# The first stage's order: a modulation half ahead of the norm's sums, first products between two modulation halves

## The chip, the cores and the metric

The kernel runs on 1 core of one Trainium2 chip. A core has TensorE (PE; its weight loads are listed apart as PEld), VectorE (DVE), ScalarE (ACT), GpSimd (POOL) and SyncE (SP), each with its own queue of instructions that it works off in order, and 16 DMA engines. The metric is the device time of one execution in microseconds; the time of a kernel is the median of its runs.

## The reference, cut to what matters

The program is one inference step of a two-layer diffusion backbone: 512 latent tokens and 128 context tokens with 1024 features go through the same weights. Both groups are modulated by their own condition vector. What the changed part computes is the very beginning of layer 0:

```python
def ada_modulation(cond, w_mod, b_mod):
    m = jax.nn.silu(cond) @ w_mod + b_mod
    return jnp.split(m, 6, axis=-1)

def modulate(h, shift, scale):
    return h * (1.0 + scale) + shift

hp = modulate(rms_norm(xp, norm_mix[l]), sh1_p, sc1_p)   # context tokens
hs = modulate(rms_norm(xs, norm_mix[l]), sh1_s, sc1_s)   # latent tokens
p = h @ w_in          # even_project: the first projection of the mixer
```

Behind it come the attention of layer 0, a SwiGLU feed-forward, layer 1 with grouped-query attention, a second feed-forward and a last norm. All inputs and outputs are float32.

## The kernel before

Activations are held transposed: 8 tiles of 128 features by 640 tokens (`x`, written x0 to x7), the tokens in two halves of 320 columns, `HALF`. The second half has 192 latent and 128 context tokens, and as the two have different conditions, its elementwise work is done in two pieces, of 192 and of 128 columns. A product at nearly float32 precision is made of three fast matmuls: an operand is split into a high part (`h`, rounded to the fast format by ScalarE) and a low part (`l`, the rest, by VectorE), and high x high, high x low and low x high are summed in PSUM (`mm3`, L181). `unit` (L168) loads a weight block of 128 x 1024 and splits it so: ScalarE's copy, then VectorE's subtraction (L173, L174).

The first stage, with the names that the profile shows:

- The norm (`nrm`, names n00...). ScalarE squares the x tiles (n00sq), VectorE adds them up (n00acc), `rstd(i)` (L215) sums over the features of half i with a matmul against ones (n00p), and ScalarE makes 1/sqrt of it by Ln and Exp (n00rs, L221 and L222).
- The modulation blocks `mod0(j)` (L353), names mod, for j = 0 to 3. A block gives shift and scale of the two feature tiles 2j and 2j+1 for both conditions. It has two halves, each of which multiplies 1 MB of weights (mraw, fetched in 2 DMAs per block) by the conditions (scol), 16 matmuls as the profile counts them; after the second half ScalarE copies the sums out of PSUM (modsb, L371), and `end()` turns them with matmuls against a selection matrix (sel) and adds the bias on VectorE (mods, L379).
- `made(j)` (L543) calls that end, makes the scale column (gs, L386) and then the modulated tiles 2j and 2j+1 for both halves: VectorE scales (h00t, L253), ScalarE adds the shift and rounds (h00h, L257), VectorE makes the low part (h00l, L258).
- `first(ks, us)` (L520) adds the products of the tiles ks with the weight blocks wA0, wA1 and wA4 (us = 0, 1, 2) to six PSUM banks, wA0a and wA0b, wA1a and wA1b, and two called wA. For one tile and one block that is 6 matmuls of 128 x 320.

The loads stand in one queue of SyncE: vectors, the 8 x tiles, block 0's two halves, wA0, block 1's two halves, wA1, wA4, the halves of blocks 2 and 3. The loads behind those (tabK, wA2, wA3 and so on) go out when buffers come free.

The order of the work is that in which the program text issues it, loosened by a scheduler that settles each engine's queue when the program is built. `run` (L115) binds its pieces: each is issued after the matmul that was written last before it. The order of this stage is written out by hand:

```python
nrm.rstd(0)
run([lambda: nrm.rstd(1)] + rows(0))
run([lambda: made(0)] + rows(1))
run([lambda: first((0, 1), [0]), lambda: made(1), lambda: first((0, 1), [1, 2])])
run(rows(2))
```

`rows(j)` (L551) are the two halves of block j. So TensorE has the norm's sums of both halves, block 0's two halves, block 0's end, block 1's two halves, the 12 products of tiles 0 and 1 with wA0, block 1's end, their 24 products with wA1 and wA4, and block 2.

Of the kernel before, what the change touches and what calls it, by code (L numbers as in the profile page):

```python
# [51 lines left out]
def body(ctx, tc, xT, vecs, crow, wm0, wm0g1, wm0g, wm1, wA, wNV, wNA, wMK, wMV, wOA, wGQ, wGK, wGV, wOC,  # L52
# [36 lines left out]
    def bank(name, kind="m"):  # L89
        if kind == "m":  # L90
            return psp.tile([P, 512], F32, tag="m", bufs=4, name=name)
        return ypool["pool"].tile([P, 512], F32, tag=kind, bufs=ypool["tags"][kind], name=name)
# [22 lines left out]
    def run(pieces):  # L115

        for piece in pieces:
            with tc.issue_after(PE.last.ins):
                piece()
# [48 lines left out]
    def unit(src, n, name, lo="v", pool=None, bufs=3):  # L168

        raw = load(src, n, name + "r")  # L170
        t = (pool or wp).tile([P, 2, 1024], F32R, tag="w", bufs=bufs, name=name)
        hi, lw = t[:, 0, :n], t[:, 1, :n]
        S.activation(hi, raw, AF.Copy)  # L173
        (V if lo == "v" else G).tensor_tensor(lw, raw, f(hi), ALU.subtract)  # L174
        return hi, lw
# [12 lines left out]
    def proj(ps, wh, wl, hh, hl, ks, c0, c1, first=True, last=True, w0=0):  # L188

        for j, k in enumerate(ks):  # L190
            a, b = wh[:, (w0 + j) * P:(w0 + j + 1) * P], wl[:, (w0 + j) * P:(w0 + j + 1) * P]
            mm3(ps[:, :c1 - c0], a, b, hh[k][:, c0:c1], hl[k][:, c0:c1], first and j == 0, last and j == len(ks) - 1)
# [160 lines left out]
    def mod0(j, bk, load_):  # L353

        box = []

        def part(half):
            def run():
                if half == 0:
                    box.append(bk())  # L360
                psm, rs = box[0], load_(j, half)

                for g in range(4):
                    for b in range(2):
                        o = 512 * (g % 2) + 256 * b
                        rows = slice(64 * b + 32 * (g % 2), 64 * b + 32 * (g % 2) + 32)
                        PE.matmul(psm[rows, :256], scol[:, 4 * half + g, :], rs[g // 2][:, o:o + 256], start=half == 0 and g < 2,
                                  stop=half == 1 and g > 1, tile_position=(0, rows.start))
                if half == 1:
                    box.append(tp.tile([P, HT], F32, tag="u", bufs=7, name=f"modsb{j}"))  # L370
                    S.activation(box[1][:, :256], psm[:, :256], AF.Copy)  # L371
            return run

        def end():
            psm, sb = box
            for i in range(2):
                PE.matmul(psm[:, 4 * i:4 * i + 4], sb[:, i * P:(i + 1) * P], sel, start=True, stop=True)
            for i, t in enumerate(MOD0[j]):
                V.tensor_tensor(mods[0][:, t:t + 2, :], psm[:, 0:8].rearrange("p (a i b) -> p a i b", a=2, b=2)[:, :, i, :],  # L379
                                bc2(bmod(0, t, 2)), ALU.add)  # L380
        return [part(0), part(1), end]

    def mkgs(l, i, k0=0, k1=8):
        sc = SC1 if i == 0 else SC2
        n = (V_NMIX if i == 0 else V_NFFN) + 8 * l
        V.scalar_tensor_tensor(gs[l][i][:, k0:k1, :], mods[l][:, sc + k0:sc + k1, :], 1.0, bc2(vec[:, n + k0:n + k1]),  # L386
                               ALU.add, ALU.mult)
# [119 lines left out]
    nrm = Norm("n00", D)  # L507
# [12 lines left out]
    def first(ks, us):  # L520
        for k in ks:
            for u in us:
                for c, (c0, c1) in enumerate(HALF):
                    proj(pss[u][c], *w3[u], hh, hl, [k], c0, c1, first=k == 0, last=k == KT - 1, w0=k)

    with tc.tile_pool(name="start", bufs=1) as big:
        raws = {}

        def fetch(j):
            for half in range(2):  # L530
                raws[j, half] = big.tile([P, 2, 1024], F32, tag="mraw", bufs=8, name=f"mraw{j}_{half}")
                nc.sync.dma_start(raws[j, half], wm0[j, 2 * half:2 * half + 2].rearrange("q p n -> p q n"))


        fetch(0)
        w3 = [unit(wA[0], 1024, "wA0")]
        fetch(1)
        w3 += [unit(wA[i], 1024, f"wA{i}") for i in (1, 4)]
        fetch(2)
        fetch(3)  # L540
        m = [mod0(j, lambda j=j: bank(f"mod{j}", "m"), lambda j, half: [raws[j, half][:, q, :] for q in range(2)]) for j in range(4)]

        def made(j):  # L543

            m[j][2]()
            mkgs(0, 0, 2 * j, 2 * j + 2)
            for k in (2 * j, 2 * j + 1):
                for i in range(2):
                    hm.make(i, nrm.rs, k)

        def rows(j):  # L551
            return m[j][:2]

        nrm.rstd(0)
        run([lambda: nrm.rstd(1)] + rows(0))
        run([lambda: made(0)] + rows(1))
        run([lambda: first((0, 1), [0]), lambda: made(1), lambda: first((0, 1), [1, 2])])
        run(rows(2))
        run([lambda: first((2, 3), [0]), lambda: made(2), lambda: first((2, 3), [1, 2])])
        run(rows(3))  # L560
        run([lambda: first((4, 5), [0]), lambda: made(3), lambda: first((4, 5), [1, 2])])
        run([lambda u=u: first((6, 7), [u]) for u in range(3)])
# [1530 lines left out]
```

## Time and profile before

| | |
|---|---|
| median of 3 runs | 1477.95 us |
| the 3 runs | 1477.95, 1478.81, 1476.01 us |
| profiled execution: span | 1475.7 us (its own time; no time around the span is listed) |
| TensorE busy | 1440.4 us, 98% |
| VectorE busy | 1235.6 us, 84% |
| ScalarE busy | 783.4 us, 53% |
| GpSimd busy | 176.0 us, 12% |
| HBM | 156 GB/s over the span; 413 GB/s from 10 to 20 us |
| first matmul of the norm's sums | at 13.52 us |
| first product of the first stage (wA0a) | at 23.72 us |
| block 2's first matmul | at 30.79 us |

Times inside the profile count from the span's start. In a timeline row stand start, duration, engine, line, operation, out<-in, the tile's size, xcount, and in brackets the idle time before it with what ended it; a row with xcount merges neighbours of one kind. A busy TensorE row overlaps the next, since matmuls are pipelined: 0.31 us is the duration of a 128 x 320 product, while such products follow each other every 0.15 us.

### The profile page before, as it was taken

The page shows a single profiled execution, that of the slowest core. Times are in us where ns is not written, and L with a number is a line of the kernel's source. Part 1 is how long each engine was busy: PE and PEld are TensorE (multiplying, and loading weights), DVE is VectorE, ACT ScalarE, POOL GpSimd, SP SyncE. Part 2 cuts the span into 40 slices and gives each one's busy share as a digit, 9 for nine tenths or more (in the row PEclk, how much of TensorE's full clock was granted, in tenths as well). Part 3 has the DMA queues.
Part 4 walks back from the last instruction along what each step waited for, and adds up shares of the span by engine and source line. Part 5 has one row for each costly group of instructions (what it writes and reads, how often), then busy time and mean ns, then how long its engine had stood idle before and what let it go on. Part 6 is the DMA issues. An engine that isn't in the chain of part 4 may idle for free.

```text
span 1475.7 us, 25826 instructions
## 1 busy us (share of the span) xinstructions
PE 1440.4 (98%) x9764; PEld 1390.5 (94%) x9764; DVE 1235.6 (84%) x2391; ACT 783.4 (53%) x1539; POOL 176.0 (12%) x270
## 2 busy tenths in 40 slices
PE   5999999999999999999999999999999999999997
PEld 3989978889999999999999999989999999999997
DVE  5877788877998889965997878888899898989976
ACT  5446677853755545531223656672656555555443
POOL 0046635420000000000000122220000000000000
PEclk9999999999999999999999999999999999999999
DMA  9643431025164555568764300115245555548572
GB/s 374 217 153 125 144 115 44 15 90 182 48 214 164 169 167 173 183 232 315 240 224 143 100 30 30 43 39 190 86 167 181 182 175 184 176 145 297 181 267 72
DMA packets 79637, 231.49 MB, mean 157 GB/s; under 512 B 8856, under 2 KB 13240, under 8 KB 79128
## 3 DMA queue, kind: packets, MB, share of 16 engines
q1 hardware_dynamic: 77152, 225.43, 44.8%
q10 hardware_dynamic: 1944, 3.48, 0.7%
q8 instruction: 76, 1.25, 0.3%
q0 software_dynamic: 416, 0.93, 0.2%
q14 instruction: 49, 0.40, 0.1%
HBM read 193.15 MB, written 36.66 MB: 156 GB/s over the span
## 4 chain that ended last, share of the span: by engine, by line
PE 75%; DVE 11%; DMA 5%; ACT 5%; issue 3%; POOL 1%; DVEq 0%; ACTq 0%; SPq 0%; POOLq 0%
PE fg L64 14%; PE fd L64 6%; PE fgo L64 5%; PE fo L64 5%; PE gq L64 4%; PE fu L64 3%; PE fdo L64 2%; PE gs L64 2%; PE go L64 2%; PE nq L64 2%; PE nk L64 1%; PE fuo L64 1%; DVE junk L1660 1%; PE gt L68 1%; DMA wm<-in_wm 1%
## 5 line engine op out<-in xcount | busy, mean ns | idle before, releaser
L1660 DVE SCALAR_TENSOR_TENSOR junk<-wm,cb 128x1024 bf16<-128x1024 f32 x88 | 107.3, 1220 | 6.7 <-DMA wm<-in_wm 5.5
L64 PE MATMUL gq<-h10h,wgq 128*128 128x320 f32 x256 | 66.3, 318 | 0.0
L267 POOL TENSOR_SCALAR h10h<-h10t,gs,mods 128x320 fp32r<-128x320 f32 x4 | 4.0, 992 | 430.8 <-DVE h10t L261 428.5
L1400 ACT ACTIVATE wY<-s 128x1024 fp32r<-128x1024 f32 x38 | 40.3, 1061 | 25.7 <-PE fg L64 21.1
L1928 POOL TENSOR_TENSOR xr<-xw,fn1rs 128x320 f32<-128x320 f32 x2 | 1.7, 858 | 412.9 <-ACT fn1rs L235 412.9
L1400 ACT ACTIVATE wZ<-s 128x1024 fp32r<-128x1024 f32 x38 | 40.1, 1055 | 15.4 <-PE fd L64 10.3
L1401 DVE TENSOR_TENSOR wZ<-s,wZ 128x1024 fp32r<-128x1024 f32 x38 | 46.3, 1220 | 1.4
L1401 DVE TENSOR_TENSOR wY<-s,wY 128x1024 fp32r<-128x1024 f32 x38 | 46.3, 1219 | 0.3
L64 PEld LDWEIGHTS gq<-h10h,wgq 128*128 128x128 f32 x256 | 45.3, 190 | 0.6
L1509 DVE TENSOR_TENSOR sg<-up,sg 128x640 f32<-128x640 f32 x38 | 31.3, 823 | 15.8 <-ACT sg L1508 14.8
L1508 ACT ACTIVATE sg<-fg 128x320 f32<-128x320 f32 x38 | 16.7, 439 | 48.4 <-PE fg L64 48.4
L64 PE MATMUL gq<-h10l,wgq 128*128 128x320 f32 x128 | 39.8, 311 | 0.0
L1530 ACT ACTIVATE p<-fd 128x320 f32<-128x320 f32 x38 | 16.6, 438 | 42.5 <-PE fd L64 42.5
L1865 ACT ACTIVATE gp<-gs,gb,rq 128x640 f32<-128x640 f32 (+1 forms) x40 | 31.8, 796 | 13.4 <-DVE gb L1864 12.0
L64 PE MATMUL fg<-h01E,wW 128*128 128x320 f32 x228 | 36.6, 309 | 1.1 <-DVE g L1540 1.1
L64 PE MATMUL fg<-h01N,wZ 128*128 128x320 f32 x228 | 36.6, 309 | 0.3 <-ACT p L1528 0.3
L64 PE MATMUL fg<-h01C,wY 128*128 128x320 f32 x228 | 36.6, 309 | 0.2 <-ACT u L1534 0.2
L64 PE MATMUL fg<-h11N,wZ 128*128 128x320 f32 x228 | 36.7, 309 | 0.0
L64 PE MATMUL fg<-h01q,wX 128*128 128x320 f32 x228 | 36.7, 309 | 0.0
L64 PE MATMUL fu<-h11q,wX 128*128 128x320 f32 x228 | 36.6, 309 | 0.0
L64 PE MATMUL fd<-h11q,wZ 128*128 128x320 f32 x228 | 36.6, 309 | 0.0
L64 PE MATMUL fd<-h01q,wZ 128*128 128x320 f32 x228 | 36.5, 309 | 0.0
(3421 smaller groups left out, 5313.5 us busy)
## 6 DMA issues: line engine op xcount, KB each, us to landing
wm<-in_wm SPq DMA_DIRECT2D x48, 512.0 KB, 4.3
mraw<-in_wm SPq DMA_DIRECT2D x8, 1024.0 KB, 13.2
mraw<-in_wm SPq DMA_DIRECT2D x14, 512.0 KB, 3.7
wmv<-in_wm0g SPq DMA_DIRECT2D x8, 512.0 KB, 4.0
wm<-in_wm0g SPq DMA_DIRECT2D x8, 512.0 KB, 5.4
ruo<-in_wFO SPq DMA_DIRECT2D x8, 512.0 KB, 4.1
rgo<-in_wFO SPq DMA_DIRECT2D x8, 512.0 KB, 5.5
x<-in_xT SPq DMA_DIRECT2D x8, 320.0 KB, 5.2
```

Of the source, the lines that this page charges most:

```text
L64: cls.last = nc.tensor.matmul(*a, **k)
L68: cls.last = nc.tensor.transpose(*a, **k)
L267: G.tensor_scalar(h[:, c0:c1], t, self.gsl[:, k, 0:1], self.ml[:, self.sh + k, 0:1], ALU.mult, ALU.add)
L1400: S.activation(h, src, AF.Copy)
L1401: V.tensor_tensor(w_, src, f(h), ALU.subtract)
L1508: last = S.activation(sg[:, 0:HT], g[:, :HT], AF.Silu, scale=-1.0)
L1509: V.tensor_tensor(sg, up, sg, ALU.mult)
L1530: S.activation(p5, b5[:, :HT], AF.Copy)
L1660: V.scalar_tensor_tensor(junk, raw, 1.0, cb[:, c, :], ALU.mult, ALU.mult, accum_out=mods[l][:, j0 + i, c:c + 1])
L1865: gexp[h, j] = S.activation(dst, src, AF.Exp, bias=nb, scale=rq[:, j:j + 1], accum_out=ll[:, j:j + 1])
L1928: G.tensor_tensor(x[k][:, c0:c1], root[1][k], nrm.rs[:, c0:c1], ALU.mult)
```

## The change

Four lines become six. The first half of block 0 is issued before the norm's sums of either half of the tokens. Block 1's second half is issued behind the six products of tile 0 with wA0, which `first((0,), [0])` makes right after block 1's first half; `first((1,), [0])` follows it with tile 1. No instruction is added, taken away or resized.

```diff
         def rows(j):
             return m[j][:2]
 
+        r0, r1 = rows(0), rows(1)
+        r0[0]()
         nrm.rstd(0)
-        run([lambda: nrm.rstd(1)] + rows(0))
-        run([lambda: made(0)] + rows(1))
-        run([lambda: first((0, 1), [0]), lambda: made(1), lambda: first((0, 1), [1, 2])])
+        run([lambda: nrm.rstd(1), r0[1]])
+        run([lambda: made(0), r1[0], lambda: first((0,), [0]), r1[1]])
+        run([lambda: first((1,), [0]), lambda: made(1), lambda: first((0, 1), [1, 2])])
         run(rows(2))
```

The queues as built differ in this stage on TensorE, ScalarE and VectorE; those of GpSimd and SyncE are the same, and so is everything behind the first 53 rows of VectorE. The numbers behind a name tell buffers apart.

**The head.** TensorE's queue from its first matmuls to block 0's selection matmuls; mraw_0 and mraw_1 are the weights of a block's first and second half. Before (-) and now (+):

```order
 L68 MATMUL cst<-ident,scol 8x128 x2
-L64 MATMUL n00p_239<-n00acc,ones 128x320
-L64 MATMUL n00p_243<-n00acc,ones 128x320
-L64 MATMUL mod_247<-mraw_0_208,scol 32x256 x8
-L64 MATMUL mod_247<-mraw_1_210,scol 32x256 x8
-L64 MATMUL mod_247<-sel,modsb_264 128x4 x2
+L64 MATMUL mod_239<-mraw_0_208,scol 32x256 x8
+L64 MATMUL n00p_248<-n00acc,ones 128x320
+L64 MATMUL n00p_252<-n00acc,ones 128x320
+L64 MATMUL mod_239<-mraw_1_210,scol 32x256 x8
+L64 MATMUL mod_239<-sel,modsb_264 128x4 x2
```

The first half of block 0 has moved ahead of both sums of the norm. ScalarE's queue at the same place, from the norm's Ln to block 0's copy and the first h00h; before:

```order
L221 ACTIVATE n00rs<-n00p_239,eps 128x320
L222 ACTIVATE n00rs<-n00rs 128x320
L221 ACTIVATE n00rs<-n00p_243,eps 128x320
L222 ACTIVATE n00rs<-n00rs 128x320
L371 ACTIVATE modsb_264<-mod_247 128x256
L173 ACTIVATE wA_214<-wA0r 128x1024
L257 ACTIVATE h00h_183<-h00t_271,mods_98 128x320
```

and now:

```order
L221 ACTIVATE n00rs<-n00p_248,eps 128x320
L222 ACTIVATE n00rs<-n00rs 128x320
L221 ACTIVATE n00rs<-n00p_252,eps 128x320
L173 ACTIVATE wA_214<-wA0r 128x1024
L222 ACTIVATE n00rs<-n00rs 128x320
L371 ACTIVATE modsb_264<-mod_239 128x256
L257 ACTIVATE h00h_183<-h00t_271,mods_98 128x320
```

The high part of wA0 (wA_214) has moved ahead of the norm's last Exp and of the copy modsb.

**The second block.** TensorE's queue from block 1's halves (mraw_0_217, mraw_1_219) to the first product of tile 1 (h00h_184); before:

```order
L64 MATMUL mod_293<-mraw_0_217,scol 32x256 x8
L64 MATMUL mod_293<-mraw_1_219,scol 32x256 x8
L64 MATMUL wA0a<-h00h_183,wA_214 128x320
L64 MATMUL wA0a<-h00l_191,wA_214 128x320
L64 MATMUL wA0a<-h00h_183,wA_214 128x320
L64 MATMUL wA0b<-h00h_183,wA_214 128x320
L64 MATMUL wA0b<-h00l_191,wA_214 128x320
L64 MATMUL wA0b<-h00h_183,wA_214 128x320
```

and now:

```order
L64 MATMUL mod_293<-mraw_0_217,scol 32x256 x8
L64 MATMUL wA0a<-h00h_183,wA_214 128x320
L64 MATMUL wA0b<-h00h_183,wA_214 128x320
L64 MATMUL wA0a<-h00l_191,wA_214 128x320
L64 MATMUL wA0a<-h00h_183,wA_214 128x320
L64 MATMUL wA0b<-h00l_191,wA_214 128x320
L64 MATMUL wA0b<-h00h_183,wA_214 128x320
L64 MATMUL mod_293<-mraw_1_219,scol 32x256 x8
```

Block 1's second half has moved behind the six products of tile 0. VectorE's queue at the end of tile 1 (h00l_192) and the start of block 1's scale and shift; wA_223 and wA_228 are the low parts of wA1 and wA4. Before:

```order
L258 SCALAR_TENSOR_TENSOR h00l_192<-h00t_286,mods_98,h00h_184 128x128
L174 TENSOR_TENSOR wA_223<-wA1r,wA_223 128x1024
L379 TENSOR_TENSOR mods_98<-mod_293,vec 128x4 x2
L386 SCALAR_TENSOR_TENSOR gs_100<-mods_98,vec 128x4
L174 TENSOR_TENSOR wA_228<-wA4r,wA_228 128x1024
L253 SCALAR_TENSOR_TENSOR h00t_329<-x_2_127,gs_100,n00rs 128x320
```

and now:

```order
L258 SCALAR_TENSOR_TENSOR h00l_192<-h00t_286,mods_98,h00h_184 128x128
L379 TENSOR_TENSOR mods_98<-mod_293,vec 128x4 x2
L386 SCALAR_TENSOR_TENSOR gs_100<-mods_98,vec 128x4
L253 SCALAR_TENSOR_TENSOR h00t_329<-x_2_127,gs_100,n00rs 128x320
L174 TENSOR_TENSOR wA_223<-wA1r,wA_223 128x1024
L258 SCALAR_TENSOR_TENSOR h00l_193<-h00t_329,mods_98,h00h_185 128x320
L253 SCALAR_TENSOR_TENSOR h00t_333<-x_2_127,gs_100,n00rs 128x192
L174 TENSOR_TENSOR wA_228<-wA4r,wA_228 128x1024
```

The low parts of wA1 and wA4 have moved behind block 1's mods and gs and behind the first one and three steps of tile 2. The low part of wA0, which stood between the first h00t and the first h00l, now stands ahead of block 0's mods.

## The prediction, on record before the changed kernel ran

> **What bounds the kernel now.** I read the busy sums first, then who waited for whom on TensorE, then the timelines of the first 33 us engine by engine. The table of stretches says that TensorE is the bound:
>
> ```profile
> 0.00:50.00 50.00, 33.91 (x282) 26.33 (x283) 29.62 (x87) 27.02 (x60) 0.70 (x6) 1.00 0.91 341
> 30.00:40.00 10.00, 10.00 (x106) 8.17 (x109) 8.07 (x26) 4.79 (x13) 0.00 (x0) 1.00 1.03 407
> 50.00:100.00 50.00, 50.00 (x270) 44.63 (x270) 45.78 (x76) 21.81 (x40) 13.27 (x26) 1.00 0.57 182
> sum 1475.70, PE 1440.38 PEld 1390.54 DVE 1235.59 ACT 783.45 POOL 175.97; mean PE 48.01 PEld 46.35 DVE 41.19 ACT 26.11 POOL 5.87
> PE n00p L64 <- DVE n00acc L212: 8.3, 1, 8.3
> ```
>
> In a row stand the stretch, its length, then the busy time of TensorE, its weight loads, VectorE, ScalarE and GpSimd with their instructions. TensorE is busy 1440.38 of 1475.70 us; of the 35.3 idle, 16.1 lie in the first 50 us (50-33.91), and from 30 us on it is busy 10.00 of 10. The changed region ends where the third modulation block starts; what counts is when that start comes, since behind it TensorE has no gap to give or take. Before it stands the start-up, where TensorE waits for VectorE, for DMA and for the split of weight block wA1. TensorE there:
>
> ```profile
> 13.52 2.50 PE L64 MATMUL n00p<-n00acc,ones 128*128 128x320 f32 x4 [8.30 <-DVE n00acc L212]
> 15.95 2.31 PE L64 MATMUL mod<-mraw,scol 128*32 128x256 f32 x32
> 18.77 0.61 PE L64 MATMUL mod<-sel,modsb 128*128 128x4 f32 x4 [0.51 <-ACT modsb L371]
> 20.25 1.07 PE L64 MATMUL mod<-mraw,scol 128*32 128x256 f32 x16 [0.87 <-DMA mraw<-in_wm]
> 22.72 1.07 PE L64 MATMUL mod<-mraw,scol 128*32 128x256 f32 x16 [1.40 <-DMA mraw<-in_wm]
> 27.38 0.41 PE L64 MATMUL wA1a<-h00h,wA 128*128 128x320 f32 x1 [0.36 <-DVE wA L174]
> 29.27 0.56 PE L64 MATMUL wA<-h00h,wA 128*128 128x320 f32 x2
> 30.79 1.93 PE L64 MATMUL mod<-mraw,scol 128*32 128x256 f32 x32
> ```
>
> Each row is start, length, what. 30.79 is the mark that I move.
>
> **Step 1, TensorE's head.** The first half of block 0 (16 matmuls) now stands ahead of the norm's sums n00p. Nothing is added; the work is the same. But TensorE works in order, so the sums now wait for that half's weights:
>
> ```profile
> 5.59 1.27 SPq L532 DMA_DIRECT2D mraw<-in_wm  x2
> mraw<-in_wm SPq DMA_DIRECT2D x1, 1024.0 KB, 8.1
> 7.88 0.34 SPq L165 DMA_DIRECT2D wA0r<-in_wA  x1
> wA0r<-in_wA SPq DMA_DIRECT2D x1, 512.0 KB, 9.7
> ```
>
> Issued at 5.59 and 8.1 us on the way, the half lands at 13.7; the sums could have begun at 13.52. So the half fills no idle TensorE time: the idle time that it was to fill ends before the data comes. What it costs depends on TensorE's speed at that moment:
>
> ```profile
> L64 PE MATMUL n00p<-n00acc,ones x4: 741/741/900, 13.5 to 15.3; 128*128 128x320 f32 x4
> L64 PE MATMUL cqp<-cqacc,ones x4: 432/432/433, 66.0 to 66.8; 128*128 128x320 f32 x4
> 65.96 1.24 PE L64 MATMUL cqp<-cqacc,ones 128*128 128x320 f32 x4
> ```
>
> The same four matmuls take 2.50 us at 13.5 and 1.24 us at 66: the array begins at half speed, although the granted clock reads 1.00 there. Both halves take 1.93 us at 30.79 and 2.31 at 15.95, so full speed came less than a microsecond into that row, at about 16.8. A half is therefore worth 0.86 us at full speed ((1.93-0.2)/2) and 1.7 at half. I take 1.7, since nothing warms the array earlier than before: 13.75+1.7 puts the sums at 15.5 instead of 13.52, +1.95; the low end is 14.6, +1.1. [...]
>
> **Step 2, ScalarE.** Its rows:
>
> ```profile
> 14.99 0.53 ACT L221 ACTIVATE n00rs<-n00p,eps 128x320 f32<-128x320 f32 x1 [2.21 <-PE n00p L64]
> 16.06 0.53 ACT L221 ACTIVATE n00rs<-n00p,eps 128x320 f32<-128x320 f32 x1
> 16.62 0.47 ACT L222 ACTIVATE n00rs<-n00rs 128x320 f32<-128x320 f32 x1
> 18.34 0.38 ACT L371 ACTIVATE modsb<-mod 128x256 f32<-128x256 f32 x1 [1.25 <-PE mod L64]
> 18.62 1.05 ACT L173 ACTIVATE wA<-wA0r 128x1024 fp32r<-128x1024 f32 x1
> 24.75 0.36 ACT L371 ACTIVATE modsb<-mod 128x256 f32<-128x256 f32 x1
> ```
>
> The first Ln follows the sums by 14.99-13.52 = 1.47, so 16.95. The split of wA0 now stands ahead of the last Exp: 16.95+1.07+0.56 = 18.58 (its weights land at 7.88+9.7 = 17.58, no wait), then 1.05+0.47 with a little overlap, and the copy modsb starts at 20.05 instead of 18.34: +1.7. TensorE's second half of block 0 (17.3 to 18.3) lies beside this. Were the sums not late, the split would wait for 17.58 and modsb still start at 19.1.
>
> **Step 3, VectorE.**
>
> ```profile
> 19.48 0.23 DVE L379 TENSOR_TENSOR mods<-mod,vec 128x4 f32<-128x4 f32 x2 [5.61 <-ACT modsb L371]
> 20.74 1.22 DVE L174 TENSOR_TENSOR wA<-wA0r,wA 128x1024 fp32r<-128x1024 f32 x1
> 21.87 0.55 DVE L258 SCALAR_TENSOR_TENSOR h00l<-h00t,mods,h00h 128x320 fp32r<-128x320 f32 x1
> 22.33 0.35 DVE L253 SCALAR_TENSOR_TENSOR h00t<-x,gs,n00rs 128x128 f32<-128x128 f32 x1
> 22.60 0.41 DVE L258 SCALAR_TENSOR_TENSOR h00l<-h00t,mods,h00h 128x192 fp32r<-128x192 f32 x1
> 22.93 0.55 DVE L253 SCALAR_TENSOR_TENSOR h00t<-x,gs,n00rs 128x320 f32<-128x320 f32 x1
> 23.65 0.68 DVE L253 SCALAR_TENSOR_TENSOR h00t<-x,gs,n00rs 128x192 f32<-128x192 f32 x2
> 24.24 1.14 DVE L258 SCALAR_TENSOR_TENSOR h00l<-h00t,mods,h00h 128x320 fp32r<-128x320 f32 x3
> 26.10 1.23 DVE L174 TENSOR_TENSOR wA<-wA1r,wA 128x1024 fp32r<-128x1024 f32 x1 [0.71 <-ACT wA L173]
> 27.24 0.22 DVE L379 TENSOR_TENSOR mods<-mod,vec 128x4 f32<-128x4 f32 x2
> 27.99 1.23 DVE L174 TENSOR_TENSOR wA<-wA4r,wA 128x1024 fp32r<-128x1024 f32 x1 [0.33 <-issue]
> ```
>
> The scale-and-shift chain now starts (mods) at 19.48+1.7 = 21.2. The wA0 split moves into the idle time before it, which saves 21.87-20.74 = 1.13 on the chain: from mods to the last h00l it took 24.24+1.14-19.48 = 5.9 less 1.13, and some 0.25 for h00l waiting on ScalarE, 5.0. It ends at 26.2 (before 25.4).
>
> **Step 4, the second block's halves.** TensorE takes the selection matmuls of block 0 at 20.5, the first half of block 1 (landed by 20.25) at 21.1 to 22.1, then the six products of tile 0. The last needs the third piece of h00l0, which ends 3.15 after mods (0.46 for the two small steps, then by VectorE's spacing in the rows, 0.46 for 320 columns, 0.33 for 192 and 0.27 for 128: 0.46+0.34+0.27+0.46+0.46+0.33, and 0.35 of its own): 24.35, products done 24.65. Only then comes the second half of block 1, which ran at 22.72: 24.65 to 25.55. Where it stood, TensorE waited for DMA; now the DMA waits for TensorE. The modsb copy of block 1 follows the last h00h: it starts 1.10 after the h00t pair at 23.65; that pair now starts 3.5 after mods, so 25.8 (before 24.75); the tile 1 products end after h00l at 26.55; the selection matmuls 26.55 to 27.1.
>
> **Step 5, the wA1 split.** VectorE did it at 26.10, ahead of the second mods; now it stands behind mods, gs and one h00t: 27.1+0.45+0.46 = 28.0, +1.9. Its first product moves from 27.38 to 29.3. The wA4 split now has h00l and h00t (0.46+0.33) ahead: 28.0+1.14+0.79 = 29.95 against 27.99, and its product 31.2 against 29.27. From there 1.52-0.15 (one product fewer behind it) to the third block: 32.6 instead of 30.79, +1.8.
>
> **What stays.** The tile 2 and 3 pieces on VectorE end at 31.1+0.27+0.33+0.46+0.26 = 32.4 and 34.1, TensorE asks for them at 34.4 and 35.3. SP and POOL keep their order; SP's loads behind the splits of wA1 and wA4 go out 2 us later:
>
> ```profile
> wA2r<-in_wA SPq DMA_DIRECT2D x1, 512.0 KB, 11.0
> 27.35 0.34 SPq L165 DMA_DIRECT2D wA2r<-in_wA  x1
> 51.88 0.31 PE L64 MATMUL ckv0a<-h00h,wA 128*128 128x320 f32 x1
> ```
>
> The first of them landed at 38.4, and its first product (ckv0a) ran at 51.88: 13 us of cover. So all 1.8 are carried to the end: span 1475.7+1.8 = 1477.5; the median of the runs stands 2.25 above that span, 1477.95+1.8 = 1479.7.
>
> **Bounds.** A half at 0.86 makes the split wait for 17.58: modsb 19.1, mods +0.75, end +0.85. Above: landing 0.3 later adds 0.3, and each of two moved VectorE splits may show the 0.33 of issue seen at 27.99: +2.7. So 1478.8 to 1480.7, and the runs spread from 1476.01 to 1478.81.
>
> **Rivals.** (a) The stall is taken up later, 1478.0. For: 35.3-16.1 leaves 19 us of idle TensorE time behind the start. Against: those waits hang on what TensorE itself started. 13 in 100. (b) The half costs the sums nothing and the early split wins. With mods back at 19.48 the chain would end 0.9 earlier, but the second half of block 1 stays tied to its DMA (22.72) and step 5's order eats the rest: modsb 24.5, wA1 split 26.0, +-0.1; if mods came 1.15 earlier, about -0.5: 1477.45. This decides if the first half lands before 13.5-1.7 = 11.8 and wA0r before 16.6; the rows say 13.7 and 17.58. 8 in 100. (c) Slower for good: TensorE, idle from 18.3 to 20.5, 22.1 to 22.8 and in pieces up to 24.3, falls back to half speed around 23.7. Until 27.1 it then does six products, a half and the selection, 0.9+0.9+0.5 = 2.3 us of work, at half speed: +2.3 more, 1482.0. For: it did run at half speed after idling up to 13.52. Against: after gaps of 0.87 and 1.40 a half still took 1.07. 6 in 100. [...]
>
> **Numbers.** The forecast holds 73 in 100. The range takes its own 1478.8 to 1480.7, the spread of the runs on either side, and (a) and (b) whole: 1476.8 to 1482. About 0.2%, 3 us, is what a measurement of this kernel can tell from no change. The forecast's 1.8 is 1.2 short of it, which run spread exceeds in one case of eight (9 in 100), (c) adds 4: slower 0.13. Faster needs (a) or (b) and a lucky median: 0.03. The same: 0.84. A slight loss, then, which the bound calls no change.
>
> **What would show it.** In the changed profile: the first mod half at about 13.75 and n00p at 15.5; n00rs at 17; modsb at 20.05; the second half of block 1 with no DMA wait at 24.7; the wA1 split behind mods at 28; the third block's matmuls at 32.6. The forecast is wrong if n00p still starts before 14.5, if the third block starts before 31.3, or if it starts late but the last layers' rows don't.

## The result and the profile after

The changed kernel is slower by a little more than forecast. In the first comparison its median was 1478.64 us against 1476.27 (17 runs each), a ratio of 1.0021 with an interval from 1.0013 to 1.0028: 3.1 us, between 1.9 and 4.1. A second comparison, with 12 runs of it, gave 1.0018 (1.0007 to 1.0029). Forecast were +1.8 us. Both ratios lie at the 0.2% that was named as the bound of what can be told from no change.

TensorE in the changed kernel's profile, as a timeline (start, duration, then as before):

```profile
13.62 1.94 PE L64 MATMUL mod<-mraw,scol 128*32 128x256 f32 x16 [8.43 <-DMA mraw<-in_wm]
15.49 2.50 PE L64 MATMUL n00p<-n00acc,ones 128*128 128x320 f32 x4
17.92 1.92 PE L64 MATMUL mod<-mraw,scol 128*32 128x256 f32 x16
22.72 0.41 PE L64 MATMUL wA0a<-h00h,wA 128*128 128x320 f32 x1 [0.76 <-ACT h00h L257]
25.07 1.76 PE L64 MATMUL mod<-mraw,scol 128*32 128x256 f32 x16
30.55 0.41 PE L64 MATMUL wA1a<-h00h,wA 128*128 128x320 f32 x1 [1.42 <-DVE wA L174]
33.84 1.50 PE L64 MATMUL mod<-mraw,scol 128*32 128x256 f32 x24
54.94 0.31 PE L64 MATMUL ckv0a<-h00h,wA 128*128 128x320 f32 x1
```

(The view of the row at 33.84 ends after 24 of the third block's 32 matmuls.)

The half of block 0 waits 8.43 us for its weights and pushes the norm's sums from 13.52 to 15.49. The second half of block 1 waits for nothing at 25.07. The third block starts at 33.84 instead of 30.79 (+3.05), and ckv0a, the first product behind the first stage, at 54.94 instead of 51.88 (+3.06): from one to the other nothing is given back. ScalarE and VectorE beside it:

```profile
16.96 0.53 ACT L221 ACTIVATE n00rs<-n00p,eps 128x320 f32<-128x320 f32 x1 [4.20 <-PE n00p L64]
18.45 1.05 ACT L173 ACTIVATE wA<-wA0r 128x1024 fp32r<-128x1024 f32 x1
19.91 0.38 ACT L371 ACTIVATE modsb<-mod 128x256 f32<-128x256 f32 x1
21.05 0.23 DVE L379 TENSOR_TENSOR mods<-mod,vec 128x4 f32<-128x4 f32 x2 [0.30 <-PE mod L64]
28.35 0.23 DVE L379 TENSOR_TENSOR mods<-mod,vec 128x4 f32<-128x4 f32 x2 [2.17 <-PE mod L64]
29.28 1.22 DVE L174 TENSOR_TENSOR wA<-wA1r,wA 128x1024 fp32r<-128x1024 f32 x1
```

Up to mods (21.05) everything stands within 0.2 us of the forecast. Block 1's mods come at 28.35 instead of the forecast 27.1, and the wA1 split behind them at 29.28 instead of 28.0. The missing 1.2 us arise between the mods of block 0 and those of block 1. The table of stretches of the same kernel shows where (the third number from the end is the granted clock of TensorE):

```profile
12.86:16.28 3.42, 2.66 (x18) 1.19 (x19) 0.99 (x3) 0.00 (x0) 0.00 (x0) 1.00 1.03 419
16.28:19.69 3.41, 3.41 (x20) 1.17 (x18) 0.16 (x1) 2.66 (x5) 0.00 (x0) 1.00 1.02 408
19.69:23.10 3.41, 2.14 (x25) 1.12 (x21) 3.04 (x9) 1.55 (x5) 0.00 (x0) 1.00 1.03 412
23.10:26.51 3.41, 3.18 (x22) 1.88 (x21) 2.81 (x9) 1.40 (x4) 0.00 (x0) 0.50 1.03 408
```

From 23.10 to 26.51 TensorE ran at a granted clock of 0.50, exactly one stretch of 3.41 us. That is rival (c), a fall back to half speed, with a smaller price than it was given. Whether it belongs to the change is what the runs had to tell.

### The profile page after: what moved, and what is told of

It is laid out like the page before. It is cut to its first block, busy times and chain, and to the rows that moved or that the text cites. A ratio compares the mean times of both kernels' runs of the same rounds, so it can differ in the third digit from the quotient of the medians.

```text
span 1478.4 us, 25827 instructions
## 1 busy us (share of the span) xinstructions
PE 1443.4 (98%) x9764; PEld 1391.4 (94%) x9764; DVE 1236.3 (84%) x2391; ACT 785.3 (53%) x1539; POOL 176.2 (12%) x270
## 4 chain that ended last, share of the span: by engine, by line
PE 84%; DVE 7%; ACT 4%; DMA 2%; issue 2%; POOL 1%; ACTq 0%; SPq 0%; DVEq 0%; POOLq 0%
PE fg L64 19%; PE fd L64 9%; PE fgo L64 5%; PE fo L64 5%; PE fu L64 4%; PE gq L64 3%; PE fdo L64 2%; PE gs L64 2%; PE go L64 2%; PE nq L64 2%; PE nk L64 1%; PE fuo L64 1%; PE gt L68 1%; PE mod L64 1%; PE gvp L64 1%
## 5 line engine op out<-in xcount | busy, mean ns | idle before, releaser
L1402 ACT ACTIVATE wY<-s 128x1024 fp32r<-128x1024 f32 x38 | 40.3, 1060 | 27.1 <-PE fg L64 22.2
L1510 ACT ACTIVATE sg<-fg 128x320 f32<-128x320 f32 x38 | 16.7, 439 | 48.3 <-PE fg L64 48.3
L1867 ACT ACTIVATE gp<-gs,gb,rq 128x640 f32<-128x640 f32 (+1 forms) x40 | 31.9, 796 | 13.2 <-DVE gb L1866 11.8
L64 PE MATMUL fg<-h11q,wX 128*128 128x320 f32 x228 | 36.5, 309 | 0.0
```

The source lines that it names most:

```text
L64: cls.last = nc.tensor.matmul(*a, **k)
L1402: S.activation(h, src, AF.Copy)
L1510: last = S.activation(sg[:, 0:HT], g[:, :HT], AF.Silu, scale=-1.0)
L1867: gexp[h, j] = S.activation(dst, src, AF.Exp, bias=nb, scale=rq[:, j:j + 1], accum_out=ll[:, j:j + 1])
```

## The experiments

The mark is the start of the third block (30.79 us before, 33.84 after). "Fall" is a stretch in which the granted clock is 0.50. The first two runs do one part of the change alone.

**The first part alone** (block 0's first half ahead of the norm's sums):

```diff
+        r0 = rows(0)
+        r0[0]()
         nrm.rstd(0)
-        run([lambda: nrm.rstd(1)] + rows(0))
+        run([lambda: nrm.rstd(1), r0[1]])
         run([lambda: made(0)] + rows(1))
```

> Only the first part of the change: block 0's first half ahead of the norm's sums; block 1's halves stand as before. The mark is the first matmul of block 2 (30.79 before, 33.84 in the changed kernel). My theory (the sums wait for the half, ScalarE's split of wA0 stands ahead of modsb): n00p at 15.5, modsb at 19.9, the split of wA1 ahead of the second mods as before, mark 31.8, +1.0. Rival 1 (all the loss is in the second part, the head is hidden by block 1's DMA wait at 22.7): mark 30.8. Rival 2 (all the loss is in the head): mark 33.8.

The mark came at 31.74, +0.95; the ratio is 1.0002 (0.9993 to 1.0011):

```profile
20.95 3.77 PE L64 MATMUL mod<-mraw,scol 128*32 128x256 f32 x32
25.72 0.37 ACT L371 ACTIVATE modsb<-mod 128x256 f32<-128x256 f32 x1
31.74 1.93 PE L64 MATMUL mod<-mraw,scol 128*32 128x256 f32 x32
```

Against the first profile of the kernel before, the late head costs about 1 us at the mark, as the steps had it. Both halves of block 1 ran at half speed here (3.77 us where 1.93 is the full-speed row), so a fall is not tied to the second part of the change. It was hidden: ScalarE came to block 1's copy at 25.72 with no idle time before it, so TensorE had the block ready in time.

**The second part alone** (tile 0's products between block 1's halves):

```diff
+        r1 = rows(1)
         run([lambda: nrm.rstd(1)] + rows(0))
-        run([lambda: made(0)] + rows(1))
-        run([lambda: first((0, 1), [0]), lambda: made(1), lambda: first((0, 1), [1, 2])])
+        run([lambda: made(0), r1[0], lambda: first((0,), [0]), r1[1]])
+        run([lambda: first((1,), [0]), lambda: made(1), lambda: first((0, 1), [1, 2])])
```

> Only the second part: the six products of tile 0 between block 1's halves; the norm's sums first, as before. My theory: n00p at 13.5 and modsb at 18.3 as before, block 1's second half at 24.0 instead of 22.7 since the products wait for h00l, the wA1 split at 27.4 instead of 26.1 since it now stands behind mods, gs and one h00t, mark 32.0 (+1.2); if TensorE also falls to half speed near 23, mark 32.8. Rival 1 (all the loss is here): 33.8. Rival 2 (all the loss is in the head): 30.8.

The theory and both rivals missed: the mark came at 35.57, +4.8, and the ratio is 1.0028 (1.0016 to 1.0040), no smaller a loss than the whole change's.

```profile
19.77 0.23 DVE L379 TENSOR_TENSOR mods<-mod,vec 128x4 f32<-128x4 f32 x2 [5.89 <-ACT modsb L371]
21.03 1.22 DVE L174 TENSOR_TENSOR wA<-wA0r,wA 128x1024 fp32r<-128x1024 f32 x1
24.85 1.94 PE L64 MATMUL mod<-mraw,scol 128*32 128x256 f32 x16
29.62 1.22 DVE L174 TENSOR_TENSOR wA<-wA1r,wA 128x1024 fp32r<-128x1024 f32 x1
30.90 0.56 PE L64 MATMUL wA1a<-h00h,wA 128*128 128x320 f32 x1 [1.63 <-DVE wA L174]
35.57 1.93 PE L64 MATMUL mod<-mraw,scol 128*32 128x256 f32 x32
```

Two things went together. Without the first part the wA0 split stays behind mods on VectorE (21.03) and lengthens the chain that tile 0's products wait for: from mods to block 1's second half it is 24.85-19.77 = 5.1 us, in the changed kernel 25.07-21.05 = 4.0. So the second part needs the 1.13 us that step 3 credited to the first. And there were two falls, 24.18 to 27.59 and 31.01 to 34.42, the second behind the wait of 1.63 us for the late wA1 split.

**Does TensorE start at half speed because it stood idle, and does keeping it busy help?** The kernel before with ten added matmuls of 128 x 320 on the x tiles ahead of the norm's sums; the results of all matmuls added in this and later runs are overwritten unread.

```diff
+    def warm(rhs):
+        PE.matmul(pss[1][1][:, :HT], ones, rhs[:, :HT], start=True, stop=True)
+    for k in (0, 1, 2, 3, 4, 5, 6, 7, 7, 7):
+        warm(x[k])
```

> The kernel before with ten extra matmuls of 128 x 320 (ones by the x tiles as they land, into columns that no one reads before they are overwritten), so that TensorE is busy from about 5 to 13 us. If the half speed at 13.5 comes from the idle time before (my theory): n00p takes 1.24 instead of 2.50 us, modsb comes at 17.6 instead of 18.34 (then block 0's second half, landing at 16.5, ends it), mark 30.1, the time 0.7 us shorter. Rival (n00p is slow for another reason, its operands or a cold program): n00p 2.5, mark 30.8. Rival (extra work delays the sums): n00p later than 13.7, mark above 30.8.

A miss again: mark 31.11, ratio 1.0007 (0.9995 to 1.0019).

```profile
4.35 5.35 PE L64 MATMUL wA1b<-x,ones 128*128 128x320 f32 x10 [4.35 <-DMA x<-in_xT]
14.04 1.34 PE L64 MATMUL n00p<-n00acc,ones 128*128 128x320 f32 x4 [0.93 <-DVE n00acc L212]
22.78 1.93 PE L64 MATMUL mod<-mraw,scol 128*32 128x256 f32 x16 [1.40 <-DMA mraw<-in_wm]
```

The norm's sums took 1.34 us instead of 2.50, near the 1.24 us of four such matmuls at 66 us in the kernel before. But the sums began 0.5 us later, behind VectorE's n00acc. Block 0's mods still came earlier (18.66 instead of 19.48), which gained nothing, since block 1's weights came no earlier: its second half waits for DMA and starts at 22.78 (22.72 before). Then that half ran at half speed (1.93 us), in an order in which the first profile of the kernel before has no fall.

**The changed kernel, looked at again:**

> The changed kernel once more, for one thing: in its first profile the matmuls from 23.4 to 26.6 ran at half speed. [...]

```profile
14.05 1.93 PE L64 MATMUL mod<-mraw,scol 128*32 128x256 f32 x16 [8.94 <-DMA mraw<-in_wm]
21.16 0.23 DVE L379 TENSOR_TENSOR mods<-mod,vec 128x4 f32<-128x4 f32 x2
24.83 1.07 PE L64 MATMUL mod<-mraw,scol 128*32 128x256 f32 x16
28.36 1.22 DVE L174 TENSOR_TENSOR wA<-wA1r,wA 128x1024 fp32r<-128x1024 f32 x1
29.63 0.42 PE L64 MATMUL wA1a<-h00h,wA 128*128 128x320 f32 x1 [1.43 <-DVE wA L174]
32.92 1.93 PE L64 MATMUL mod<-mraw,scol 128*32 128x256 f32 x32
```

No fall in the first stage this time: the half of block 1 took 1.07 us at 24.83 (forecast 24.65), the split came at 28.36 (28.0), the mark at 32.92 (32.6). Against the first profile of the kernel before, the order alone costs 32.92-30.79 = 2.1 us at the mark; the fall of the first profile added 33.84-32.92 = 0.9.

**The wA1 split put back** ahead of block 1's mods, in the changed kernel (`unit.lo` is VectorE's subtraction; `made(1)` is issued after that of wA1):

```diff
-        (V if lo == "v" else G).tensor_tensor(lw, raw, f(hi), ALU.subtract)
+        unit.lo = (V if lo == "v" else G).tensor_tensor(lw, raw, f(hi), ALU.subtract)
...
-        w3 += [unit(wA[i], 1024, f"wA{i}") for i in (1, 4)]
+        w3 += [unit(wA[1], 1024, "wA1")]
+        lo1 = unit.lo
+        w3 += [unit(wA[4], 1024, "wA4")]
...
-        run([lambda: first((1,), [0]), lambda: made(1), lambda: first((0, 1), [1, 2])])
+        run([lambda: first((1,), [0]), lambda: after(lo1, lambda: made(1)), lambda: first((0, 1), [1, 2])])
```

> The changed kernel, and VectorE's split of wA1 put back ahead of block 1's mods (block 1's end is issued after it). Nothing else moves but the h00h and the wA4 split that follow it. My theory (this order is a term of its own in the loss): against the changed kernel's second profile, where TensorE kept its speed (wA1 split at 28.36, mark 32.92), the split comes at 27.3 and the mark at 31.85, 1.1 earlier; if TensorE falls to half speed near 23 as in the first profile, 32.8 instead of 33.84. Rival (the order is only a symptom, block 1's late second half sets the mark whatever the order is): mark unchanged, 32.9 or 33.8.

```profile
27.44 1.23 DVE L174 TENSOR_TENSOR wA<-wA1r,wA 128x1024 fp32r<-128x1024 f32 x1 [1.13 <-ACT wA L173]
28.72 0.42 PE L64 MATMUL wA1a<-h00h,wA 128*128 128x320 f32 x1 [0.41 <-DVE wA L174]
32.12 1.93 PE L64 MATMUL mod<-mraw,scol 128*32 128x256 f32 x32
```

TensorE's wait for the split shrank from 1.42 to 0.41 us, the mark came at 32.12 although there was a fall from 21.15 to 24.57, and the ratio is 1.0003 (0.9994 to 1.0012). Step 5 of the prediction, the split's place, is thus about 1 us of the loss at the mark, and with it undone no loss in time is clear of the noise.

**The same mend on the second part alone** (the two diffs above, without the first part):

> The second part alone (products between block 1's halves), with the wA1 split put back ahead of block 1's mods. My theory: the loss of the second part is for the most part that split's place and a fall of TensorE's speed. At full speed the mark comes at 31.3 (0.5 behind before), with a fall near 23 at 32.3; in the run of the second part alone it was 35.57 with two falls. Rival (the loss is that the products hold up block 1's second half, and no order behind it helps): mark 32.0 without, 33 and more with a fall; time ratio still above 1.002.

The theory missed, the rival was met: mark 33.90, ratio 1.0027 (1.0016 to 1.0038). The half of block 1 came at 25.86 and took 1.94 us, in a double fall from 22.80 to 29.62, and the split waited for ScalarE until 29.22. Without the first part the loss is the same with the split in either place (1.0027 and 1.0028). The products hold up block 1's second half here; how much of that is the order and how much the double fall, the run does not separate.

**The gaps filled**: the changed kernel with 4 added matmuls of 128 x 128 in two idle places, behind block 0 and behind block 1's first half (`fill(n)` issues n of them).

```diff
-        run([lambda: nrm.rstd(1), r0[1]])
-        run([lambda: made(0), r1[0], lambda: first((0,), [0]), r1[1]])
+        run([lambda: nrm.rstd(1), r0[1], lambda: fill(2)])
+        run([lambda: made(0), r1[0], lambda: fill(2), lambda: first((0,), [0]), r1[1]])
```

> The changed kernel with four extra matmuls of 128 x 128 in two of TensorE's gaps, two behind block 0's second half and two behind block 1's first half; ScalarE's and VectorE's queues stay. [...] Rival (the fall has nothing to do with the gaps): it is there in some executions as before, the ratio stays at 1.002 or grows with the extra work.

```profile
26.09:29.50 3.41, 2.04 (x14) 1.69 (x12) 2.20 (x7) 2.24 (x4) 0.00 (x0) 1.00 1.02 402
29.50:32.91 3.41, 3.33 (x12) 3.33 (x13) 3.41 (x9) 1.66 (x4) 0.00 (x0) 0.50 1.03 407
```

The fall between 20 and 27 us was gone, but another came at 29.50, behind the wait of 1.42 us for the wA1 split; mark 34.20, ratio 1.0014 (1.0005 to 1.0024). One profile does not show that the filling did either: the unfilled changed kernel, looked at again, has no fall between 20 and 27 us either, and the interval holds the unfilled 1.0021 and 1.0018.

**The kernel before, filled**: 24 matmuls of 128 x 128 ahead of the sums and 6 in two gaps.

```diff
+    run([lambda k=k, n=n: fill(n, x[k]) for k, n in ((0, 2), (1, 2), (2, 2), (3, 3), (4, 3), (5, 3), (6, 3), (7, 6))])
...
-        run([lambda: nrm.rstd(1)] + rows(0))
-        run([lambda: made(0)] + rows(1))
+        r1 = rows(1)
+        run([lambda: nrm.rstd(1)] + rows(0) + [lambda: fill(2)])
+        run([lambda: made(0), r1[0], lambda: fill(4), r1[1]])
```

> The kernel before with TensorE kept busy: 24 extra matmuls of 128 x 128 on the x tiles as they land (behind the small transposes this time), two behind block 0's second half, four between block 1's halves, all where TensorE waits. My theory: n00p in 1.3 us at 13.5, modsb at 17.6, no fall of speed, mark 30.1, and a time below before's by 0.7 us or by some more, since before too loses speed in some executions: 0.9990 to 0.9996. Rival (half speed at the start costs nothing, since DMA sets block 1): mark 30.8, ratio 1.000.

```profile
8.14 7.14 PE L64 MATMUL wA1b<-x,ones 128*128 128x128 f32 x40 [1.22 <-DMA x<-in_xT]
15.12 1.24 PE L64 MATMUL n00p<-n00acc,ones 128*128 128x320 f32 x4
```

The theory missed. The fill itself ran at half speed up to 13.2 us (421 ns for a matmul there, 275 behind it) and held the sums up to 15.12; mark 31.13, ratio 1.0005 (0.9996 to 1.0014). There was no fall in the first stage, and still no gain.

**The kernel before, looked at again.** This run tells whether the changed order alone brings the fall.

> The kernel before, looked at once more. If the second half-speed stretch of TensorE is something that the changed order alone brings, both halves of block 1 take 1.07 us each again and the third block starts at 30.8 (within 0.2). If it is a matter of the execution, as the two profiles of the changed kernel (33.84 and 32.92 us) suggest, before has it in some executions as well: then the second half of block 1 takes over 1.5 us and the third block starts at 31.3 to 32.

Timeline, and the table of stretches of the same execution:

```profile
15.87 3.60 PE L64 MATMUL mod<-mraw,scol 128*32 128x256 f32 x32
20.69 0.23 DVE L379 TENSOR_TENSOR mods<-mod,vec 128x4 f32<-128x4 f32 x2 [6.91 <-ACT modsb L371]
23.00 1.94 PE L64 MATMUL mod<-mraw,scol 128*32 128x256 f32 x16 [1.39 <-DMA mraw<-in_wm]
25.96 0.36 ACT L371 ACTIVATE modsb<-mod 128x256 f32<-128x256 f32 x1
27.30 1.23 DVE L174 TENSOR_TENSOR wA<-wA1r,wA 128x1024 fp32r<-128x1024 f32 x1 [0.71 <-ACT wA L173]
31.98 1.93 PE L64 MATMUL mod<-mraw,scol 128*32 128x256 f32 x32
53.08 0.31 PE L64 MATMUL ckv0a<-h00h,wA 128*128 128x320 f32 x1
```

```profile
12.48:15.89 3.41, 2.45 (x8) 1.20 (x8) 1.30 (x4) 1.22 (x3) 0.00 (x0) 1.00 1.02 418
19.31:22.72 3.41, 1.79 (x24) 0.99 (x20) 1.96 (x6) 2.24 (x4) 0.00 (x0) 1.00 1.03 411
22.72:26.13 3.41, 3.13 (x21) 1.86 (x22) 3.41 (x10) 1.79 (x5) 0.00 (x0) 0.50 1.02 405
```

The kernel before falls as well, from 22.72 to 26.13. A fall depends on the execution, not on the order alone.

The third block starts at 31.98 here instead of 30.79, but this fall is not the reason. Full speed came late, at 19.31 instead of 16.77: the halves of block 0 took 3.60 us instead of 2.31, and mods came at 20.69 instead of 19.48. That is already the whole 1.2 us. From mods to the wA1 split it is 27.30-20.69 = 6.61 us with the fall and 26.10-19.48 = 6.62 without, to the mark 11.29 and 11.31. The fall was hidden as in the first part alone: ScalarE had no idle time before block 1's copy (25.96).

In the changed kernel it is the other way round. Its mods come at 21.05, 21.16 and 21.04 in three profiles in which full speed came at 19.69, 17.35 and 17.95, so a late full speed costs it nothing, and the fall costs it 0.9 us.

**The second part alone, looked at again:**

> The second part alone, looked at once more. If the order alone (products ahead of block 1's second half, split of wA1 behind the second mods) made most of the 4.8 us by which its third block came late, it starts late again at 34.5 or later, even where all matmuls run at full speed. If the half-speed stretches made it (24.08 to 27.4 and 30.9 to 34.2 us), an execution without them shows 32.5 to 33.5.

There were three stretches at half speed (22.61 to 29.44 in two, then 32.85 to 36.26), the third block started at 36.91, and ckv0a came at 58.01, against 56.66 in its first profile and 51.88 before. An execution of it without a fall was not seen, so how much of its loss the order alone makes stays open.

**Both mends together**: the changed kernel with the split put back and the two gaps filled.

> The changed kernel with both mends: the wA1 split ahead of block 1's mods, and four added matmuls (128 columns, their result overwritten unread) in two gaps. If the loss is the split's order plus the fall to half speed, the third block starts at 31.5 to 32.0, the first product behind the whole first stage at 52.6 to 53.1, and the ratio to the kernel before is 1.000 to 1.001. If the added matmuls only move the fall on, as they did with the split behind (29.6 to 32.7 us), half speed shows again between 27 and 33 us, the third block starts at 32.5 or later and the ratio is 1.001 to 1.002. If the parts that are left give something back, as a rival to both, the start is 30.5 to 31 and the ratio under 1.000.

```profile
31.98 1.93 PE L64 MATMUL mod<-mraw,scol 128*32 128x256 f32 x32
```

No fall in the whole first stage, the mark at 31.98, the ratio 1.0000 (0.9991 to 1.0009). That is the mark of the first expectation. It is 1.2 us behind the first profile of the kernel before and level with the second, which also has 31.98. The mean granted clock of its runs is the highest of all kernels timed (0.9975 in the table below). No version beats the kernel before.

**The changed kernel, timed again:**

> The changed kernel, timed once more. Paired by whether TensorE falls to half speed in the start-up, the profiles so far put the changed order at 54.01-51.88 = 2.1 us (no fall in either) and 54.94-53.08 = 1.9 us (a fall in both) behind the kernel before. If that is the whole loss and the falls come as often in both kernels, the ratio is 1.0012 to 1.0015 (1.8 to 2.2 us). If the changed order also falls more often or for longer, it is 1.0018 to 1.0025 again, as in the first comparison (1.0021). The profile shows the third block at 32.6 to 33.1 us without a fall and at 33.6 to 34 with one.

The ratio of 1.0018 (1.0007 to 1.0029) is the lower end of the second theory, and its interval holds both. The profile has two falls in the first stage, one more than either theory had thought of, and the mark at 35.73:

```profile
24.78:28.19 3.41, 3.41 (x22) 2.17 (x23) 1.11 (x4) 2.08 (x4) 0.00 (x0) 0.50 1.02 408
28.19:31.60 3.41, 1.78 (x13) 1.53 (x12) 2.66 (x7) 1.51 (x2) 0.00 (x0) 1.00 1.02 406
31.60:35.02 3.42, 3.42 (x15) 3.42 (x14) 3.42 (x9) 1.81 (x5) 0.00 (x0) 0.50 1.02 400
56.82 0.31 PE L64 MATMUL ckv0a<-h00h,wA 128*128 128x320 f32 x1
```

So ckv0a starts at 54.01, 54.94 or 56.82 in the changed kernel with none, one or two falls in the first stage. In the kernel before it starts at 51.88 with an early full speed and at 53.08 with a late one, whose fall cost nothing. The expectation paired 54.94 with 53.08 as "a fall in both"; their difference of 1.9 us is 54.01-53.08 = 0.9 for the order and 0.9 for a fall that only the changed kernel pays for.

## Where the loss comes from

**The order: 0.9 to 2.1 us, by when full speed comes.** The changed kernel without a fall has ckv0a at 54.01. That is 2.1 us behind the kernel before where full speed came at 16.77 (51.88), and 0.9 behind it where it came at 19.31 (53.08). The reason is the head. In the seven profiles with block 0's half first, mods come at 21.04 to 21.19; in the five with the norm's sums first and no added matmuls, at 19.48 to 20.72, since there the half speed delays them. Of the 2.1 us about half is thus the late head (0.95 at the mark in the first part alone, which is 31.74 against 30.79, but no loss against 31.98), and about half the place of the wA1 split (32.92 in the changed kernel against 31.98 with the split put back and the gaps filled, neither with a fall: 0.9).

**Falls: the rest.** Over the executions whose span and clock are on record, 89 of the kernel before and 30 of the changed one, the mean spans are 1474.3 and 1477.3 us, +3.0. The order leaves 0.9 to 2.1 us of this to the falls. Two things can make them up:

- Falls are dearer. The fall of the first stage cost the changed kernel 33.84-32.92 = 0.9 us and the kernel before nothing, as shown above.
- There are more of them. A stretch at half speed takes 0.5*3.41 us off the mean granted clock, 0.0012 of it over 1476 us. The mean clocks are 0.9967 and 0.9957, so the changed kernel has 0.001/0.0012 = 0.9 such stretches more per execution (0.4 to 1.4 by the scatter of the runs). A stretch that isn't hidden cost 0.9 to 1.6 us in the profiles (the latter is 129.5-127.9, at the end of this text), which makes an estimate of 0.8 to 1.4 us.

The mean clock does not tell where in the 1476 us the falls lie. The three profiles of the changed kernel have three such stretches in the first stage and four behind it, the two of the kernel before have one and two. So the share of the falls in the 3.0 us is an estimate, and how it divides stays open.

Why more often? The wait of 1.4 to 1.6 us for the late wA1 split is a new gap. Of the six profiles with the split behind mods, four have a fall that begins between 29 and 33 us (the second part alone twice, the changed kernel filled, and the changed kernel timed again); of the eight with the split ahead of them, none has. In the four the wait lies within one stretch, which was busy 52 to 60%. In one of the two others it lies across the edge of two (76 and 82%), in the other within one of 58%, which no fall followed. With the split put back the mean clock is 0.9965, about that of the kernel before. That the gap is the cause is thus supported but not shown; it was not tried with the gap alone, without the split's delay.

| kernel | runs | mean span, us | mean clock | ratio to before |
|---|---|---|---|---|
| before | 89 | 1474.3 | 0.9967 | |
| changed | 30 | 1477.3 | 0.9957 | 1.0021, 1.0018 |
| first part alone | 10 | 1474.7 | 0.9964 | 1.0002 |
| second part alone | 11 | 1478.9 | 0.9942 | 1.0028 |
| second part, split first | 6 | 1478.3 | 0.9942 | 1.0027 |
| changed, split first | 10 | 1474.5 | 0.9965 | 1.0003 |
| changed, filled | 11 | 1476.4 | 0.9962 | 1.0014 |
| changed, split first, filled | 11 | 1474.1 | 0.9975 | 1.0000 |

The two slowest kernels have the lowest clock. The runs of a row include the single executions looked at again; the ratios are those of the timed comparisons.

## Why the prediction was right, and where it was not

**Step 1** held: the sums came at 15.49 (15.5 forecast, +1.97). The weights landed at 13.62 to 14.05, and the half took 1.94 us at half speed, 1.87 from start to start (1.7). That full speed comes at 16.8 was true of one execution only; in the five profiles of the two kernels it came at 16.77 to 19.69 us. A late full speed costs the changed kernel nothing (mods at 21.05 with 19.69, 21.16 with 17.35), but the mods and the mark of the kernel before move by 1.2 us with it, and step 1 did not ask for that. The mark of 30.79 from which all is counted is that of an early one.

**Step 2** held: n00rs 16.96 (16.95), modsb 19.91 (20.05). **Step 3** held: mods 21.05 (21.2), with the wA0 split at its place ahead of them; the 1.13 us saved there are what the second part alone lacks.

**Step 4**: the second half of block 1 behind the products, without a DMA wait, at 24.83 without a fall and 25.07 with one (24.65). **Step 5**: the wA1 split behind mods at 28.36 without a fall (28.0), 29.28 with one; the mark at 32.92 (32.6), 33.84 and 35.73. The order's term was put at 1.8 and measured 2.1 against the execution from which it was worked out, and 0.9 against the one with a late full speed. Without a fall the 0.3 above the forecast arise between the mods of block 0 (21.16, forecast 21.2) and those of block 1 (27.43, forecast 27.1). **What stays** held up to ckv0a: 54.94-33.84 = 21.10 us, before 51.88-30.79 = 21.09. Rival (a), that the stall is taken up later, did not happen there, nor behind it: the last feed-forward's last product starts at 1328.1 us against 1325.3 (two stretches at half speed lie behind the first stage in each of these profiles), and the total of 3.0 us is no smaller than the order's 0.9 to 2.1. Rival (b) is refuted with its condition: the weights landed at 13.62, not at 11.8.

**The term that was mis-sized is rival (c).** It stood outside the sum, with 6 chances in 100 and +2.3 us. It was met in two of the changed kernel's three profiles, costing 0.9 us once and, with a second fall, 35.73-32.92 = 2.8; on the average it is within the 0.9 to 2.1 us that the order leaves. For the 23.7 us at which it put the fall the prediction names no run; the first profile has the fall from 23.10 to 26.51. The argument against it failed: "after gaps of 0.87 and 1.40 a half still took 1.07" was one execution: the kernel before, looked at again, has a half of 1.94 us behind a gap of 1.39. Nor did a long gap precede the fall: in the changed kernel's first profile the stretch ahead of it, 19.69 to 23.10, has no gap over 0.76 us and is busy for 2.14 of 3.41 us.

**The base** was off as well: the forecast set 1.8 us on a median of three runs, 1477.95, and the median of the 89 executions is 1475.9. The forecast of 1479.7 stands so near the measured 1478.6 (first comparison) and 1479.9 (second) because a base 2 us too high and a loss 1.2 us too small partly cancel; that nearness is luck. The loss is the number to judge by.

## What to carry to other kernels

An order can be costed row by row against one profile to a few tenths of a microsecond. What TensorE's clock does cannot, because it differs between executions of the same program: two profiles of the kernel before are 1.2 us apart at the mark. Before blaming a change for half-speed matmuls, look at the granted clock in a second profile of both kernels. Then follow a delay from row to row before putting it down to a fall: a half that runs slowly may lie beside another engine's work and cost nothing. When work is moved ahead on one engine, look at what it moves behind on the others: here a split that fell behind the next block's small steps cost 0.9 us at the mark and opened a gap.

## What was not expected of the hardware

**A grid of 3.413 us.** In the profiles of this case the falls of an execution begin and end on one grid, whose step is their own length, 3.41 us. In the first profile of the kernel before there are two, far behind the first stage (a last one begins at 1470.84, behind TensorE's last matmul, as in every profile at its end):

```profile
204.50:207.91 3.41, 3.41 (x16) 3.41 (x17) 2.85 (x12) 2.28 (x10) 0.61 (x2) 0.50 0.00 0
866.69:870.10 3.41, 3.41 (x15) 3.37 (x14) 2.07 (x6) 2.04 (x5) 0.00 (x0) 0.50 0.08 34
```

From one start to the other it is 662.2 us, 194 times 3.413 (in the changed kernel from 23.10 to 207.42 it is 184.32 us, 54 times 3.413). From 204.50 back, 55 steps lead to 16.77, where full speed came: block 0's halves, 2.31 us instead of 1.93, put it at 15.95+2*0.38 = 16.7. The phase differs from execution to execution: full speed came at 16.77, 17.35, 17.95, 19.31 and 19.69 in the five profiles of the two kernels. In the last two of these the stretch in which TensorE began was busy 2.45 and 2.66 of 3.41 us (12.48 and 12.86 in the rows above) and did not bring it; the next, full one did. The granted clock reads 1.00 during that first half speed (12.86 to 19.69 above, where a half took 1.94 us) and 0.50 only in later falls, so the start must be read from durations.

**What makes a fall is not the busy share alone.** In the first stage no stretch at full speed that was busy over 72% was followed by a fall, all of those under 55% were, and between them both happened: 57 and 62% without one in the kernel before, 63% (2.14 of 3.41) with one in the changed kernel. What else counts was not found. With two gaps filled a fall came at a third (29.50 above), and the matmuls added at the start of the kernel before themselves ran at half speed (421 ns instead of 275) up to 13.2 us and gained nothing in time (1.0005; with the ten wider ones 1.0007).

**The falls explain part of the scatter.** From the last modulation block to the feed-forward's first matmul (191.5 to 376.4 us in the first profile of the kernel before) it took 183.8 us without a fall, 184.9 with one stretch at half speed and 186.6 in the changed kernel's first profile with two, 207.42 to 214.25. A fall at 867 made the 256 rows of gq 129.5 us long instead of 127.9. A second scatter, 465.6 to 469.3 us for the feed-forward between these places, shows no fall and stays open.
